# A two-layer RWKV-7 and neighbourhood-attention trunk: ungated heads, spread scalings, a tile of its own for the last scaling

## The chip, the cores and the metric

The kernel runs on one core of one Trainium2 chip. The metric is device time in microseconds (us): the median of several runs of the whole program, less being better. Beside the runs there is one execution recorded by the hardware profiler, and every duration and wait below comes from that recording.

The engines go by short names: PE is TensorE (matmuls and transposes), PEld its weight loads, DVE is VectorE, ACT is ScalarE, POOL is GpSimd, SP is SyncE, and SPq in a row is SP's queue that issues DMAs. Each engine works through its own list of instructions strictly in order; engines wait for each other by semaphores. SBUF is the on-chip memory that tiles live in, PSUM the banks that PE writes its sums to.

## What is computed

Two samples of 512 tokens and 1024 features (the prompt, s=0, and the sample, s=1) go through the same two layers. Cut to what matters here:

```python
def _trunk(x, ...):
    for i in range(DEPTH):                       # 2 layers
        xn = _rms_norm(x, pre_norm_g[i])
        h = _rwkv7_branch(xn, ...) if i % 2 == 0 else _natten_branch(xn, ...)
        x = x + _rms_norm(h, post_norm_g[i])
    return x

def _natten_branch(xn, w_in, b_in, rpb, w_o, b_o):
    q, k, v, z = jnp.split(xn @ w_in + b_in, 4, axis=-1)
    o = _neighbourhood_attention(q * HEAD_DIM ** -0.5, k, v, rpb)   # 16 heads of 64
    return (o * jax.nn.silu(z)) @ w_o + b_o
```

The gate `silu(z)` multiplies the attention's output elementwise, before the output product with `w_o`. The RMS norm after it needs the sum of squares over all 1024 features of a token, so the last scaling of a sample can't begin before its last output column is there.

## The kernel before

**Products.** Every large product is made in fp32 out of pairs of rounded halves: the operand x is `hi + lo`, and one 128x512 step of a product is three matmuls (hi·hi, hi·lo, lo·hi; L429 to L431 in `gemm`). Eight steps, 24 matmuls, make one output column of 128 features for 512 tokens. The weights arrive as raw tiles by DMA (three buffers, `NRAW`), ACT casts each to its `hi` half (L378) and DVE subtracts to get `lo` (L379, both in `halves`); four buffers each hold the halves of the streamed weights.

**Order.** The first part of the program, to about 1075 us, holds the recurrent scans and the first layer's products and is ordered by hand; the change leaves its order alone. What follows is emitted as interleaved Python generators and put in order by the framework's scheduler, which simulates the engines and takes the ready instruction of the highest priority; `high_priority(n)` and `later(n)` shift that priority, and `behind(a, b)` orders instruction a after b. The DMA issues of SP are ordered in the same way, loads and stores in one queue.

**The second layer**, for a sample s:

- `inproj`/`qkvz`: for each of eight pairs of heads p, four columns q, k, v, z. A column is summed in one of two PSUM banks, `pg`. For s=1 DVE moves it out of the bank, multiplied by the norm's factor `x1_rstd` (held in `vs`; L1380), ACT adds the bias (L1384, L1386, L1388, or for z a tanh and an identity, L1391 and L1392), DVE makes the gate (L1394), and SP stores the column to DRAM. At the end of s=1 the columns come in the order q6 k6 v6 q7 k7 v7 z6 z7.
- `heads(s, p)`: loads q, k, v and the bias; v is transposed (L1413, copied by ACT at L1414); for two halves of the queries, scores into one of two PSUM banks `sc` (L1427), softmax on DVE and ACT (L1437 to L1443, the exponential being ACT's L1441), transposes of the probabilities into one of two PSUM banks `pt` (L1447), copies of these to `pts` by ACT (L1450), and the product with v back into the same `sc` bank (L1471). Before the second half's product the generator stays put until column z of this pair has been emitted. Then L1485 multiplies the result straight out of PSUM by z, which SP has loaded (`z<-dz`). For s=1 the gated output is split into halves (`os`).
- `out1(0)`: sample 0's output product: eight columns of 24 matmuls; then the norm (`rstd`, L460 to L469), and for each of eight columns a load of the residual `xr`, the scaling (L1511), the addition (L1512) and the store of y (L1513). PE works by then on sample 1's columns.
- `by_token`: sample 1's residual is transposed (L1523), copied (L1525) and stored.
- `last()`: sample 1's output product with tokens on the partitions, so that the norm is along a row: all 16 tiles of `w_ao` are loaded and split first, then for two halves c of the features and four groups m of tokens 24 matmuls (L1565 to L1567). `LAST[m]` gives the bank, `pg` or `pt` by turns. DVE adds the bias (L1569), ACT squares and sums (L1570), DVE multiplies by the norm's weight in place (L1571); for c=1 then the two sums (L1574), square root (L1575), reciprocal (L1576), two scalings with the residual added (L1578), and two stores by SP (L1579).

Tiles that matter below: `tmp` is a rotating set of five 128x512 buffers, and `oa` and `os` hold columns through the end. A tile may be written again only when its last reader has finished.

Of the kernel before, what the change touches and what calls it, by code (L numbers as in the profile page):

```python
# [10 lines left out]
F32 = mybir.dt.float32  # L11
# [7 lines left out]
P = 128  # L19
T = 512  # L20
# [217 lines left out]
class Trunk:  # L238
    NACT, NW, NRAW, NXR, NTMP, WP = 18, 4, 3, 3, 5, 512
    POST0, POST, POST2, POST3, NPA = 0.7, 1.0, 0.15, 0.66, 5  # L240
    HP, HS = (1000, 0), 1000
# [13 lines left out]
    NA = 1000  # L255
    SUMS, SG, ZY = 0, 0, 2
# [119 lines left out]
    def halves(self, src, lo, hi, eng=None):  # L376

        self.nc.scalar.copy(hi, src)  # L378
        (eng or self.nc.vector).tensor_tensor(lo, src, hi.bitcast(F32), op=ALU.subtract)  # L379
        return hi, lo  # L380
# [907 lines left out]
    def norm0(self, s):  # L1288

        nc = self.nc  # L1290
        rstd = self.h_acc
        yield from self.rstds(rstd)
        acc = self.t("vs", bufs=self.NVS)
        for k in range(KT):
            h = self.h[k]
            x = self.load(self.t("xr", bufs=self.NXR), self.a["xc"][s][k * P:(k + 1) * P, :])
            nc.vector.scalar_tensor_tensor(h, h, self.vec("post0", k), rstd, op0=ALU.mult, op1=ALU.mult)
            nc.vector.tensor_tensor(h, h, x, op=ALU.add)
            nc.scalar.activation(x, h, AF.Square)
# [73 lines left out]
    def qkvz(self, s, p, c, ps):  # L1373
# [4 lines left out]
        if s:  # L1378
            yield first("D")
            vt.tensor_tensor(o, ps, self.x1_rstd, op=ALU.mult)  # L1380
# [16 lines left out]
    def heads(self, s, p):  # L1397
# [19 lines left out]
        left, z = [], []  # L1417
        for ns in ((0, 1), (2, 3)):
# [34 lines left out]
            if ns[1] == 3:  # L1453
                while ("z1", s, p) not in self.sp:
                    yield
# [22 lines left out]
            left.append((sc, slice(ns[0] * P, ns[0] * P + 2 * P)))  # L1478
            yield
            if ("z1", s, p) in self.sp:  # L1480
                if not z:
                    z.append(self.load(b("z1"), self.sp["z1", s, p]))
                for sc, at in left:
                    with self.tc.high_priority(self.HP[s] if p == NP - 1 else 0):
                        vt.tensor_tensor(  # L1485
                            o[:, at].rearrange("p (n t) -> p n t", n=2), sc[:, :, 2 * NKEY:],
                            z[0][:, at].rearrange("p (n t) -> p n t", n=2), op=ALU.mult)
                left = []
# [7 lines left out]
    def out1(self, s):  # L1496
        nc = self.nc
        x = self.operands(lambda k: self.os[s][k])
        acc = self.t("acc1", pool=self.ap)
# [8 lines left out]
        rstd = self.rstd(acc)  # L1508
        for k, h in enumerate(hs):
            x = self.load(self.t("xr", bufs=self.NXR), self.sp["x1", s, k])  # L1510
            nc.vector.scalar_tensor_tensor(h, h, self.vec("post1", k), rstd, op0=ALU.mult, op1=ALU.mult)  # L1511
            (nc.vector if k % 2 else nc.vector).tensor_tensor(h, h, x, op=ALU.add)  # L1512
            nc.sync.dma_start(self.a["y"][s][k * P:(k + 1) * P, :], h)  # L1513
            yield
# [14 lines left out]
    def last(self):  # L1529
# [27 lines left out]
        for c in range(2):  # L1557
            cs = slice(c * T, c * T + T)
            for m in range(4):
# [3 lines left out]
                for k in range(KT):  # L1563
                    (xh, xl), (wh, wl) = self.os[1][k], w[c][k]
                    nc.tensor.matmul(ps, xh[:, ms], wh, start=(k == 0), stop=False)  # L1565
                    nc.tensor.matmul(ps, xh[:, ms], wl, start=False, stop=False)
                    nc.tensor.matmul(ps, xl[:, ms], wh, start=False, stop=(k == KT - 1))  # L1567
                hs[c, m] = h = self.t("oa", (P, T), NP, F32, self.ap)
                vt.tensor_tensor(h, ps, row["bo"][:, cs], op=ALU.add)  # L1569
                act.activation(self.tmp(), h, AF.Square, accum_out=st[:, m, c:c + 1])  # L1570
                (vt if c and m == 3 else vt).tensor_tensor(h, h, row["post1"][:, cs], op=ALU.mult)  # L1571
                if c:
# [4 lines left out]
                    for j in range(2):  # L1577
                        vt.scalar_tensor_tensor(hs[j, m], hs[j, m], r, xt[j], op0=ALU.mult, op1=ALU.add)  # L1578
                        nc.sync.dma_start(self.a["y"][1][ms, j * T:j * T + T], hs[j, m])  # L1579
# [343 lines left out]
```

## Time and profile before

| what | value |
|---|---|
| runs | 1678.75, 1676.94, 1675.66 us |
| their median | 1676.94 us |
| the profiled execution | 1671.44 us |
| its span, first to last instruction | 1669.6 us |
| mean granted TensorE clock of the span | 0.961 |
| DMA over the span | 326.86 MB, mean 196 GB/s |

How to read the profile: a row of a timeline gives the start, the duration, the engine, the line of the kernel, what it wrote and read, how many instructions it holds, and in square brackets for how long the engine had been idle and what it waited for. Matmuls overlap, so the step from one start to the next is a matmul's cost, not its duration. A row of the windows gives, for a stretch of the span, each engine's busy time and instructions, the clock granted to PE as a share of full speed, and the DMA engines' busy share. A row of the waits gives: the waiting engine, tile and line, what it waited for, the total, the number of times, and the longest. Some matmul records are missing, so counts in windows are lower bounds.

### The profile page before, as it was taken

What the parts mean: (1) busy time and instruction counts of PE and PEld (TensorE: products, weight loads), DVE (VectorE), ACT (ScalarE), POOL (GpSimd) and SP (SyncE); (2) the same over time, 40 slices, a digit from 0 to 9 for tenths busy, and PEclk for the clock granted to TensorE, in tenths of its full rate; (3) what the DMA queues carried; (4) which work ended last, traced back from release to release, by engine and by line L of the source; (5) the groups of instructions that cost most, each with busy time, mean ns of one, the idle gap of its engine ahead of it and who ended that gap; (6) DMA issues with size and microseconds to landing.
All of it is one profiled execution on the core that took longest, in us unless ns stands there. A gap on an engine that the chain in (4) does not pass through costs nothing.

```text
span 1669.6 us, 46734 instructions
## 1 busy us (share of the span) xinstructions
PE 1523.9 (91%) x19072; PEld 1168.3 (70%) x19072; DVE 1183.1 (71%) x2661; ACT 968.5 (58%) x2001; POOL 20.6 (1%) x64
## 2 busy tenths in 40 slices
PE   7989777987998898889889989999999999999988
PEld 6867555765665676676667766788777787777766
DVE  8985788777887887968788987343456686555654
ACT  5444665756757575566856555444566665454552
POOL 0000000000000000000000000000000000000000
PEclk9989987998999999999899999999999999999999
DMA  5435786777775767768774656574565347655552
GB/s 210 164 126 178 239 285 204 220 228 240 223 227 190 215 217 238 231 191 254 217 234 158 219 172 212 162 242 159 172 197 176 93 145 249 190 166 172 157 159 101
DMA packets 247096, 326.86 MB, mean 196 GB/s; under 512 B 54849, under 2 KB 132801, under 8 KB 246881
## 3 DMA queue, kind: packets, MB, share of 16 engines
q1 hardware_dynamic: 246880, 323.87, 61.0%
q8 instruction: 150, 2.46, 0.6%
q14 instruction: 66, 0.53, 0.1%
HBM read 220.37 MB, written 103.42 MB: 194 GB/s over the span
## 4 chain that ended last, share of the span: by engine, by line
PE 48%; DVE 10%; ACT 9%; DMA 5%; issue 3%; SPq 1%; DVEq 0%; ACTq 0%
PE pg L430 6%; PE pg L429 6%; PE pg L431 6%; PE pm L763 5%; PE pm L764 4%; PE pm L765 4%; DMA cab<-dab 2%; PE sc L1471 2%; PE pf L1080 2%; PE sc L1427 1%; PE pt L1447 1%; PE zy L1157 1%; PE us L1171 1%; DVE ab L844 1%; PE zy L1126 1%
## 5 line engine op out<-in xcount | busy, mean ns | idle before, releaser
L763 PE MATMUL pm<-act,whi 128*128 128x512 f32 x608 | 269.5, 443 | 21.1 <-ACT act L746 14.7
L764 PE MATMUL pm<-act,whi 128*128 128x512 f32 x608 | 247.5, 407 | 15.5 <-DVE act L748 14.0
L765 PE MATMUL pm<-act,wlo 128*128 128x512 f32 x608 | 245.5, 404 | 0.3 <-DVE wlo L726 0.2
L429 PE MATMUL pg<-act,whi 128*128 128x512 f32 x480 | 192.9, 403 | 2.8 <-DVE tmp L1380 1.9
L430 PE MATMUL pg<-act,whi 128*128 128x512 f32 x480 | 191.4, 399 | 0.0
L431 PE MATMUL pg<-act,wlo 128*128 128x512 f32 x480 | 190.8, 398 | 0.0
L379 DVE TENSOR_TENSOR wlo<-raw,whi 128x512 fp32r<-128x512 f32 x156 | 107.0, 688 | 86.1 <-ACT whi L378 81.2
L378 ACT CAST whi<-raw 128x512 fp32r<-128x512 f32 x156 | 96.4, 618 | 114.6 <-PE pg L430 68.5
L763 PEld LDWEIGHTS pm<-act,whi 128*128 128x128 f32 x608 | 118.2, 194 | 62.4 <-ACT act L746 17.0
L764 PEld LDWEIGHTS pm<-act,whi 128*128 128x128 f32 x608 | 119.1, 196 | 42.0 <-DVE act L748 19.0
L726 DVE TENSOR_TENSOR wlo<-raw,whi 128x512 fp32r<-128x512 f32 x152 | 103.3, 686 | 56.4 <-ACT whi L724 56.2
L765 PEld LDWEIGHTS pm<-act,wlo 128*128 128x128 f32 x608 | 118.7, 195 | 28.2 <-DVE wlo L726 2.1
L724 ACT CAST whi<-raw 128x512 fp32r<-128x512 f32 x152 | 92.6, 619 | 77.6 <-PE pm L764 65.6
L429 PEld LDWEIGHTS pg<-act,whi 128*128 128x128 f32 x480 | 90.6, 189 | 21.5 <-DVE tmp L1380 2.1
L430 PEld LDWEIGHTS pg<-act,whi 128*128 128x128 f32 x480 | 90.8, 189 | 19.4 <-issue 2.0
L431 PEld LDWEIGHTS pg<-act,wlo 128*128 128x128 f32 x480 | 90.7, 189 | 19.5 <-issue 1.7
L970 DVE TENSOR_TENSOR N<-etmp,N 128x30 f32<-128x30 f32 (+14 forms) x240 | 79.8, 333 | 8.2
L1080 PE MATMUL pf<-cab 64*64 64x128 f32 (+1 forms) x2048 | 72.0, 271 | 12.1 <-issue 6.6
L969 DVE TENSOR_TENSOR etmp<-N 128x30 f32<-128x30 f32 (+14 forms) x240 | 78.2, 326 | 3.4
L1166 ACT COPY X<-zy 64x256 f32<-64x256 f32 x128 | 46.9, 366 | 46.8 <-PE zy L1157 41.1
L1441 ACT ACTIVATE sb<-sb,mx 128x192 f32<-128x192 f32 x128 | 57.1, 449 | 24.7 <-DVE mx L1440 24.5
L1080 PEld LDWEIGHTS pf<-cab 64*64 64x64 f32 x2048 | 57.6, 136 | 18.7 <-issue 8.9
(400 smaller groups left out, 3188.5 us busy)
## 6 DMA issues: line engine op xcount, KB each, us to landing
dab<-ab SPq DMA_DIRECT2D x32, 1024.0 KB
cab<-dab SPq DMA_DIRECT2D x64, 512.0 KB
raw<-in_w_in_dram SPq DMA_DIRECT2D x128, 256.0 KB
raw<-in_w_z_dram SPq DMA_DIRECT2D x32, 256.0 KB
dz<-tmp SPq DMA_DIRECT2D x32, 256.0 KB
raw<-in_w_k_dram SPq DMA_DIRECT2D x32, 256.0 KB
dk<-tmp SPq DMA_DIRECT2D x32, 256.0 KB
raw<-in_w_r_dram SPq DMA_DIRECT2D x32, 256.0 KB
```

Of the source, the lines that this page charges most:

```text
L378: self.nc.scalar.copy(hi, src)
L379: (eng or self.nc.vector).tensor_tensor(lo, src, hi.bitcast(F32), op=ALU.subtract)
L429: nc.tensor.matmul(ps, hi, x[k][0], start=(k == 0), stop=False)
L430: nc.tensor.matmul(ps, hi, x[k][1], start=False, stop=False)
L431: nc.tensor.matmul(ps, lo, x[k][0], start=False, stop=(k == KT - 1))
L724: nc.scalar.copy(hi, raw[h])
L726: nc.vector.tensor_tensor(lo, raw.pop(h), hi.bitcast(F32), op=ALU.subtract)
L763: nc.tensor.matmul(ps, hi[:, at], xh, start=(k == 0), stop=False)
L764: nc.tensor.matmul(ps, hi[:, at], xl, start=False, stop=False)
L765: nc.tensor.matmul(ps, lo[:, at], xh, start=False, stop=(k == KT - 1))
L970: vt.tensor_tensor(N[:, q + 1:, :q], tv, N[:, q + 1:, :q], op=ALU.add)
L1080: end = nc.tensor.matmul(f[half(1 - a), h, 0, d, g] if st.last else f[half(1 - a), h, :, d, g], ab[half(h), d, g, 2 * e[d] + a], rt if st. ...
```

## The change

Five things, all after 1075 us:

1. **Heads without their gate leave PSUM ungated.** `heads` no longer waits for column z between the two halves. If z has not been emitted when a half's product is there, ACT copies the product out of `sc` as it is, and one multiply over all 512 columns follows in SBUF once z is there. Otherwise the multiply out of PSUM stays.
2. **Sample 0's last scalings are spread.** `out1(0)` waits until three of sample 1's columns have been moved out of PSUM; each load, scaling, addition and store is then given a lower priority (`OUT_LATER`), and each scaling is ordered behind the latest such move (`self.evac`).
3. **The last scaling has its own tile.** For c=1, the square writes its unused elementwise result into the PSUM bank instead of a `tmp`; the multiply by the norm's weight writes to a `tmp` rather than in place, for c=1. The first matmul of the two last groups is ordered behind the end of the group before. The very last store is issued by ACT.
4. Sample 0's last pair of heads (p=7) gets priority 3000 in place of 1000.
5. `norm0`'s scalings from the second on are ordered behind the split of sample 0's operands (`self.joint`).

```diff
-    HP, HS = (1000, 0), 1000
+    HP, HS = (3000, 0), 3000
+    OUT_LATER = 1500
...
-            nc.vector.scalar_tensor_tensor(h, h, self.vec("post0", k), rstd, op0=ALU.mult, op1=ALU.mult)
+            normed = nc.vector.scalar_tensor_tensor(h, h, self.vec("post0", k), rstd, op0=ALU.mult, op1=ALU.mult)
+            if k:
+                self.behind(normed, self.joint)
...
-            vt.tensor_tensor(o, ps, self.x1_rstd, op=ALU.mult)
+            self.evac = vt.tensor_tensor(o, ps, self.x1_rstd, op=ALU.mult)
+            self.did["evac"] += 1
...
-            if ns[1] == 3:
-                while ("z1", s, p) not in self.sp:
-                    yield
...
+            at = slice(ns[0] * P, ns[0] * P + 2 * P)
+            ov, gate = (x[:, at].rearrange("p (n t) -> p n t", n=2) if x is not None else None for x in (o, z()))
+            with self.tc.high_priority(self.HP[s] if p == NP - 1 else 0):
+                if gate is None:
+                    act.copy(ov, sc[:, :, 2 * NKEY:])
+                    left.append(at)
+                else:
+                    vt.tensor_tensor(ov, sc[:, :, 2 * NKEY:], gate, op=ALU.mult)
+        while left and z() is None:
+            yield
+        if left:
+            at = slice(left[0].start, left[-1].stop)
+            with self.tc.high_priority(self.HP[s] if p == NP - 1 else 0):
+                vt.tensor_tensor(o[:, at], o[:, at], z()[:, at], op=ALU.mult)
...
         rstd = self.rstd(acc)
+        while self.did["evac"] < 3:
+            yield
         for k, h in enumerate(hs):
-            x = self.load(self.t("xr", bufs=self.NXR), self.sp["x1", s, k])
-            nc.vector.scalar_tensor_tensor(h, h, self.vec("post1", k), rstd, op0=ALU.mult, op1=ALU.mult)
-            (nc.vector if k % 2 else nc.vector).tensor_tensor(h, h, x, op=ALU.add)
-            nc.sync.dma_start(self.a["y"][s][k * P:(k + 1) * P, :], h)
+            with self.later(self.OUT_LATER):
+                x = self.load(self.t("xr", bufs=self.NXR), self.sp["x1", s, k])
+                self.behind(nc.vector.scalar_tensor_tensor(h, h, self.vec("post1", k), rstd, op0=ALU.mult, op1=ALU.mult), self.evac)
+                nc.vector.tensor_tensor(h, h, x, op=ALU.add)
+                nc.sync.dma_start(self.a["y"][s][k * P:(k + 1) * P, :], h)
...
+                    if c and m > 1 and k == 0:
+                        self.behind(begun, ended)
...
-                act.activation(self.tmp(), h, AF.Square, accum_out=st[:, m, c:c + 1])
-                (vt if c and m == 3 else vt).tensor_tensor(h, h, row["post1"][:, cs], op=ALU.mult)
+                act.activation(ps if c else self.tmp(), h, AF.Square, accum_out=st[:, m, c:c + 1])
+                hs[c, m] = self.tmp() if c else h
+                vt.tensor_tensor(hs[c, m], h, row["post1"][:, cs], op=ALU.mult)
...
-                        nc.sync.dma_start(self.a["y"][1][ms, j * T:j * T + T], hs[j, m])
+                        (act if m == 3 and j else nc.sync).dma_start(self.a["y"][1][ms, j * T:j * T + T], hs[j, m])
```

What it does to the built order is shown at two places. Line numbers of the changed kernel are a little higher: L379 becomes L380, L1380 becomes L1383, L1511 and L1512 become L1526 and L1527, L1441 becomes L1451, L1450 becomes L1460; L1490 is the new copy.

**The middle, on DVE**, where sample 0's output product has ended and sample 1's first columns run (`os` are sample 0's eight output columns, `wlo` the halves of the next weights, the `pg` banks hold columns k0 and v0). Before:

```order
L379 TENSOR_TENSOR wlo_18739<-raw_18732,whi_18738 128x512
L1511 SCALAR_TENSOR_TENSOR os_18125<-os_18125,cv,acc_3095_18080 128x512
...
L1511 SCALAR_TENSOR_TENSOR os_18496<-os_18496,cv,acc_3095_18080 128x512
L1512 TENSOR_TENSOR os_18125<-os_18125,xr_18596 128x512
L1512 TENSOR_TENSOR os_18176<-os_18176,xr_18649 128x512
L1512 TENSOR_TENSOR os_18238<-os_18238,xr_18699 128x512
L379 TENSOR_TENSOR wlo_18803<-raw_18798,whi_18802 128x512
L1380 TENSOR_TENSOR tmp_18669<-pg_18621,vs_18182 128x512
L1380 TENSOR_TENSOR tmp_18725<-pg_18686,vs_18182 128x512
```

And in the changed kernel, the same place:

```order
L380 TENSOR_TENSOR wlo_18724<-raw_18717,whi_18723 128x512
L380 TENSOR_TENSOR wlo_18788<-raw_18783,whi_18787 128x512
L1383 TENSOR_TENSOR tmp_18659<-pg_18616,vs_18182 128x512
L1383 TENSOR_TENSOR tmp_18710<-pg_18676,vs_18182 128x512
L1526 SCALAR_TENSOR_TENSOR os_18125<-os_18125,cv,acc_3095_18080 128x512
L380 TENSOR_TENSOR wlo_18792<-raw_18785,whi_18791 128x512
L1527 TENSOR_TENSOR os_18125<-os_18125,xr_18746 128x512
L380 TENSOR_TENSOR wlo_18898<-raw_18893,whi_18897 128x512
L1383 TENSOR_TENSOR tmp_18775<-pg_18727,vs_18182 128x512
L1526 SCALAR_TENSOR_TENSOR os_18176<-os_18176,cv,acc_3095_18080 128x512
```

The two moves out of `pg` stood behind eight scalings and three additions; now they stand ahead of all of them, and one scaling and one addition follow each later move. On SP's queue the eight stores of y, which stood within 25 rows, are spread over 53 in the same way, each among the loads of weights.

**The tail, on PE**, where the last pair of heads (1,7) meets the last columns (`sc_20928`/`sc_20929` is the second half of pair (1,6); `sc_21139`/`sc_21129` the first half of pair (1,7); `pg_21366`/`pg_21367` is the first sum of `last()`). Before, the second half of pair 6, then z6's last steps and the whole of z7, 18 matmuls of `last()`, and only then the scores:

```order
L1471 MATMUL sc_20928<-pts_20963,vtok_20784 64x64
L431 MATMUL pg_21011<-act_18531,wlo_21008 128x512
...
L1567 MATMUL pg_21366<-act_21300,os_20756 128x512
L1427 MATMUL sc_21139<-k_3762_21102,q_3761_21100 64x192 x8
L1427 MATMUL sc_21201<-k_3762_21102,q_3761_21100 64x192 x8
```

In the changed kernel the scores stand within z6 and z7:

```order
L1437 MATMUL sc_21129<-k_3762_21097,q_3761_21095 64x192
L1478 MATMUL sc_20929<-pts_21019,vtok_20784 64x64
...
L1437 MATMUL sc_21129<-k_3762_21097,q_3761_21095 64x192 x7
L432 MATMUL pg_21012<-act_18527,wlo_21009 128x512
...
L432 MATMUL pg_21079<-act_18511,wlo_21072 128x512
L1437 MATMUL sc_21202<-k_3762_21097,q_3761_21095 64x192 x8
L430 MATMUL pg_21079<-act_18515,whi_21071 128x512
```

The first scores of pair 7 moved up by 43 matmuls of 512 columns, the second by 30.

**The tail, on ACT**, where the halves of the last tiles of `w_ao` are cast (`whi_213..`, the 13th to 16th of 16) and pair 7's probabilities are copied to `pts`. Before:

```order
L378 CAST whi_21360<-raw_21361 128x512
L1441 ACTIVATE sb_21149,mx_21150<-sb_21149,mx_21150 128x192
...
L1441 ACTIVATE sb_21230,mx_21237<-sb_21230,mx_21237 128x192
L1450 COPY pts_21165<-pt_21148 128x384
L1450 COPY pts_21184<-pt_21167 128x384
L1450 COPY pts_21227<-pt_21210 128x384
L1450 COPY pts_21246<-pt_21229 128x384
```

In the changed kernel, where the eight exponentials stand further up, among the casts of the sixth to tenth tile:

```order
L1460 COPY pts_21166<-pt_21138 128x384
L1460 COPY pts_21185<-pt_21168 128x384
L379 CAST os_21064<-tmp_20810 128x512
L379 CAST whi_21343<-raw_21344 128x512
L379 CAST whi_21349<-raw_21350 128x512
L379 CAST whi_21355<-raw_21356 128x512
L379 CAST whi_21361<-raw_21362 128x512
L1460 COPY pts_21228<-pt_21211 128x384
L1460 COPY pts_21247<-pt_21230 128x384
```

All of pair 7's exponentials and half of its copies now stand ahead of the last casts, and the other half of the copies still behind them. In the whole program the ungated way out (two copies L1490, one multiply L1499) is taken by pair (1,6) alone.

More of the change, by code (lines that the diff above doesn't have):

```diff
@@ L378, in halves @@
         self.nc.scalar.copy(hi, src)
-        (eng or self.nc.vector).tensor_tensor(lo, src, hi.bitcast(F32), op=ALU.subtract)
+        self.parted = (eng or self.nc.vector).tensor_tensor(lo, src, hi.bitcast(F32), op=ALU.subtract)
         return hi, lo
@@ L1416, in heads, with z @@
         o = self.tmp() if s else self.t("oa", (P, T), NP, F32, self.ap)
-        left, z = [], []
+        left, gates = [], []
+        def z():
+            if not gates and ("z1", s, p) in self.sp:
+                gates.append(self.load(b("z1"), self.sp["z1", s, p]))
+            return gates[0] if gates else None
         for ns in ((0, 1), (2, 3)):
@@ L1477, in heads @@
                                 self.behind(av, first)
-            left.append((sc, slice(ns[0] * P, ns[0] * P + 2 * P)))
             yield
[L1480 to L1488, printed above, removed]
+            at = slice(ns[0] * P, ns[0] * P + 2 * P)
[12 more added lines that the diff above has]
+                vt.tensor_tensor(o[:, at], o[:, at], z()[:, at], op=ALU.mult)
         with self.tc.high_priority(self.HP[s] if p == NP - 1 else 0):
@@ L1498, in out1 @@
         x = self.operands(lambda k: self.os[s][k])
+        self.joint = self.parted
         acc = self.t("acc1", pool=self.ap)
@@ L1564, in last @@
                     (xh, xl), (wh, wl) = self.os[1][k], w[c][k]
-                    nc.tensor.matmul(ps, xh[:, ms], wh, start=(k == 0), stop=False)
+                    begun = nc.tensor.matmul(ps, xh[:, ms], wh, start=(k == 0), stop=False)
+                    if c and m > 1 and k == 0:
+                        self.behind(begun, ended)
                     nc.tensor.matmul(ps, xh[:, ms], wl, start=False, stop=False)
-                    nc.tensor.matmul(ps, xl[:, ms], wh, start=False, stop=(k == KT - 1))
+                    ended = nc.tensor.matmul(ps, xl[:, ms], wh, start=False, stop=(k == KT - 1))
                 hs[c, m] = h = self.t("oa", (P, T), NP, F32, self.ap)
                 vt.tensor_tensor(h, ps, row["bo"][:, cs], op=ALU.add)
-                act.activation(self.tmp(), h, AF.Square, accum_out=st[:, m, c:c + 1])
-                (vt if c and m == 3 else vt).tensor_tensor(h, h, row["post1"][:, cs], op=ALU.mult)
+                act.activation(ps if c else self.tmp(), h, AF.Square, accum_out=st[:, m, c:c + 1])
+                hs[c, m] = self.tmp() if c else h
+                vt.tensor_tensor(hs[c, m], h, row["post1"][:, cs], op=ALU.mult)
                 if c:
```

## The prediction

> **What bounds the kernel now.** I read the page's first part, then the windows, the waits of PE from 1050 us on, and the timelines at the waits. First the page, and six windows of 10 us (PE, PEld, DVE, ACT, POOL, granted clock, DMA share, GB/s):
>
> ```profile
> PE 1523.9 (91%) x19072; PEld 1168.3 (70%) x19072; DVE 1183.1 (71%) x2661; ACT 968.5 (58%) x2001; POOL 20.6 (1%) x64
> ```
> ```profile
> 1380.00:1390.00 10.00, 10.00 (x57) 8.55 (x55) 7.73 (x15) 4.42 (x8) 0.00 (x0) 1.00 0.49 160
> 1390.00:1400.00 10.00, 8.13 (x34) 6.43 (x33) 6.62 (x11) 4.61 (x8) 0.00 (x0) 0.83 0.89 312
> 1410.00:1420.00 10.00, 9.01 (x49) 7.43 (x48) 7.29 (x40) 8.46 (x26) 0.00 (x0) 1.00 0.60 189
> 1610.00:1620.00 10.00, 8.07 (x58) 5.77 (x59) 8.98 (x36) 7.16 (x19) 0.00 (x0) 1.00 0.51 151
> 1620.00:1630.00 10.00, 8.42 (x54) 6.50 (x54) 2.81 (x17) 2.93 (x10) 0.00 (x0) 0.83 0.07 23
> 1660.00:1670.00 10.00, 2.20 (x10) 1.45 (x8) 3.96 (x8) 1.01 (x3) 0.00 (x0) 0.72 0.28 105
> ```
>
> PE sets the time. Where it is full, as at 1380, only fewer matmuls would help, and the change takes none away; it can win only where PE falls short: the five other rows. What PE waits for there, by tile and line (total, times, longest):
>
> ```profile
> PE sc L1427 <- DVE tmp L1485: 2.4, 1, 2.4
> PE pg L429 <- DVE tmp L1380: 1.9, 1, 1.9
> PE pt L1447 <- DVE sb L1443: 1.5, 3, 1.1
> PE pt L1447 <- ACT pts L1450: 1.4, 1, 1.4
> ...
> PE pt L1523 <- ACT tmp L1525: 1.0, 1, 1.0
> ...
> PE pt L1413 <- DMA v<-dv: 0.7, 1, 0.7
> ```
>
> The second and fifth of these lie in the middle, at 1394 and 1416; the others in the tail, 1600 to 1625. After PE's last matmul comes the end, 1662 to 1670.
>
> **Part 1, the spread scalings (middle).** The timeline of DVE, then that of PE:
>
> ```profile
> 1385.63 5.39 DVE L1511 SCALAR_TENSOR_TENSOR os<-os,cv,acc 128x512 f32<-128x512 f32 x8 [0.84 <-ACT acc L469]
> 1390.93 1.90 DVE L1512 TENSOR_TENSOR os<-os,xr 128x512 f32<-128x512 f32 x3
> ...
> 1393.34 1.29 DVE L1380 TENSOR_TENSOR tmp<-pg,vs 128x512 f32<-128x512 f32 x2
> ```
> ```profile
> 1391.62 0.60 PE L1523 MATMUL pt<-cc,hh 128*128 128x128 f32 x4
> 1394.09 0.50 PE L429 MATMUL pg<-act,whi 128*128 128x512 f32 x1 [1.87 <-DVE tmp L1380]
> ...
> 1394.66 0.54 PE L431 MATMUL pg<-act,wlo 128*128 128x512 f32 x1
> ...
> 1398.53 0.40 PE L429 MATMUL pg<-act,whi 128*128 128x512 f32 x1
> 1398.77 0.39 PE L430 MATMUL pg<-act,whi 128*128 128x512 f32 x1
> ```
>
> Eight scalings and three additions, 5.39 + 1.90 = 7.29 us, stand in DVE's queue ahead of the two moves out of `pg`. Both banks are full, so column z0 waits 1.87 us for the first move. Then PE is slow: the 10 steps from 1394.66 to 1398.53 take 3.87 us, 0.39 each, against 0.24 for the step at 1398.53. At 0.23 (the tail's steps, below) they would be 2.3 us: 1.57 us lost to the clock after the wait. In the new order both moves stand ahead of the first scaling, so the wait goes (1.87), and with it, I take it, the slow stretch (1.57). The third term is the wait of 0.99 us at 1416, where a transpose finds its bank not yet copied by ACT:
>
> ```profile
> 1416.50 0.66 PE L1523 MATMUL pt<-cc,hh 128*128 128x128 f32 x4 [0.99 <-ACT tmp L1525]
> ```
>
> ACT is then at 8.46 of 10 with the softmax of sample 1's first pair. That work starts some 3 us earlier in the new order, the transposes being spread out further, so I count the wait as gone. Sum: 1.87 + 1.57 + 0.99 = 4.4 us; if ACT is as crowded as before, 3.4; if only the wait itself is won, 1.9.
>
> What is moved costs this. The 16 scalings and additions, 0.67 us each by the row of eight (5.39 / 8), now come one pair a column behind a move: 1.3 us of DVE for each column of 24 x 0.23 = 5.5 us. DVE is at 7.7 of 10 in the full window at 1380, with eight scalings partly in it; queued behind such a pair are the halves of the next weights, held back by at most 1.3 us, and four buffers stand between these and PE. Cover enough: nothing. The loads of `xr` and stores of y on SP's queue are moved too: each store waits for its addition, and raw weights stand behind it. That is a rival below. The DMA share of 0.89 at 1390 to 1400 rather falls when the stores spread.
>
> [...]
>
> **Part 2, ungated heads (tail).** PE's timeline, with the DVE and DMA rows that released it:
>
> ```profile
> 1607.50 0.34 SPq L334 DMA_DIRECT2D z<-dz  x1
> ```
> ```profile
> 1607.91 0.40 PE L1567 MATMUL pg<-act,os 128*128 128x512 f32 x1
> 1610.71 1.53 PE L1427 MATMUL sc<-k,q 64*64 64x192 f32 x32 [2.41 <-DVE tmp L1485]
> ...
> 1619.49 0.97 PE L1447 MATMUL pt<-cc,sb 128*128 128x128 f32 x4 [1.07 <-DVE sb L1443]
> 1620.64 0.44 PE L1447 MATMUL pt<-cc,sb 128*128 128x128 f32 x2 [0.18 <-DVE sb L1443]
> 1622.48 0.55 PE L1447 MATMUL pt<-cc,sb 128*128 128x128 f32 x3 [1.40 <-ACT pts L1450]
> ...
> 1624.79 0.78 PE L1565 MATMUL pt<-h,os 128*128 128x512 f32 x1
> ...
> 1626.98 0.39 PE L1567 MATMUL pt<-h,os 128*128 128x512 f32 x1
> ...
> 1661.81 0.40 PE L1567 MATMUL pt<-whi,os 128*128 128x512 f32 x1
> ```
>
> Pair 7's scores wait 2.41 us for `sc`, which pair 6 holds until z6 has gone to DRAM and come back. Then its softmax and copies come late, and PE waits 1.07 + 0.18 + 1.40 us. With the 0.7 for v (the last row of the waits): 5.7 us. At 1624.79 starts the sum in a `pt` bank. From the order, 150 of the 192 matmuls of `last()` are left then, and 12 small products. The five steps to 1626.98 take 2.19 us, 0.44 each, double the rest: (1661.81 - 1626.98) is 34.83 us for 145 - 1 steps and the products, of some 1.2 us: 0.23 each. So 2.19 - 5 x 0.23 = 1.0 us more is lost to the clock.
>
> After the change the same PE work stands ahead of that `pt` sum (42 matmuls of `last()`, 16 score matmuls, 12 transposes, 12 products in either order). If nothing waited but v, PE would be there at 1624.79 - 5.06 - about 1 (slow steps on the way) = 1618.7. But ACT frees `sc` now: a copy of 128x256 out of PSUM is
>
> ```profile
> L1185 ACT COPY y<-zy 128x256 f32<-128x256 f32 x32 | 11.8, 369 | 5.5 <-PE zy L1175 5.1 <-DVE AK L1059 0.3
> ```
>
> 0.37 us, and the second of these stands behind two or three casts that wait for raw tiles; I take 0.6 us of wait for PE. And the bank itself: it is free only when `pts` has been copied, and that copy stands behind the casts of tiles 13 to 16:
>
> ```profile
> 1590.37 0.62 ACT L378 CAST h<-raw 128x512 fp32r<-128x512 f32 x1 [4.11 <-DMA raw<-in_w_ao_dram]
> ...
> 1616.98 0.62 ACT L378 CAST whi<-raw 128x512 fp32r<-128x512 f32 x1 [1.08 <-DMA raw<-in_w_ao_dram]
> ```
> ```profile
> L1441 ACT ACTIVATE sb<-sb,mx 128x192 f32<-128x192 f32 x128 | 57.1, 449 | 24.7 <-DVE mx L1440 24.5
> ```
>
> The 16 tiles come through three raw buffers, one each (1616.98 - 1590.37) / 15 = 1.77 us, a cast being 0.62: ACT and DVE hold the buffer, the load fills it, and any wait of ACT is passed on to the next load. Ahead of the last cast now stand, beyond what stood there before, eight exponentials (8 x 0.45 = 3.6 us), two copies to `pts` and two ungated copies (some 1.6 us): 5.2 us. All of it in ACT's waits for raw tiles would cost nothing, and the cast ends at 1617.6 as before; all of it in series, 1622.8. I take two thirds, since the exponentials in turn wait for DVE: 1621.1. The first copy to `pts` ends 0.5 us later, and the sum starts at 1621.6 instead of 1624.79: **3.2 us**. PE then waits some 2 to 3 us ahead of it, as long as the waits that are gone, so the 1.0 us of slow steps stays. Bounds: 0 (cast at 1624.3) to 6.1 + 1.0.
>
> **Part 3, the end.** The last columns' rows on DVE, and SP's:
>
> ```profile
> 1662.24 0.69 DVE L1569 TENSOR_TENSOR oa<-pt,rbo 128x512 f32<-128x512 f32 x1 [1.31 <-PE pt L1567]
> 1663.78 0.69 DVE L1571 TENSOR_TENSOR oa<-oa,rpost 128x512 f32<-128x512 f32 x1 [0.85 <-ACT tmp L1570]
> 1664.39 0.15 DVE L1574 TENSOR_TENSOR st<-st 128x1 f32<-128x1 f32 x1
> ```
> ```profile
> 1660.29 6.58 SPq L1579 DMA_DIRECT2D out_dram<-oa  x4
> ```
>
> L1571 writes in place and so waits for ACT's square to have read. With a tile of its own it runs beside the square, and L1574 comes when the square is done, 1663.78 rather than 1664.39: **0.6 us**. The square's write to PSUM has no row; its nearest is any ACT row, and I take 0 (-0.1 to 0.1). The last store, issued by ACT beside SP: I take 0 (-0.3 to 0.3), since SP's issues end with the span in either case.
>
> **Parts 4 and 5.** Sample 0's last pair and `norm0`: the order around them hardly moves, and PE has no wait there in the list: 0 (-0.3 to 0.3).
>
> **Sum:** 4.4 + 3.2 + 0.6 = 8.2 us. The profiled execution of 1671.44 becomes 1663.2. The median of the runs shown, 1676.94, is 5.5 us above it; I keep that distance: **1668.7 us**.
>
> **The rivals.**
> - *The tail's stream isn't slowed.* ACT has the room (7.16 of 10 at 1610): the exponentials fit in its waits. Then PE is at the `pt` sum at 1618.7 with no wait, or 0.6 later: 5.5 to 6.1, and the slow steps go, 1.0. Total 4.4 + 6.8 + 0.6 = 11.8: 1665.1. Chance 0.15.
> - *The clock isn't won in the middle.* The slow steps come of something else than the wait, say of the transposes and the thin PE work around it, which stay. Then part 1 is 2.9 and the total 6.7: 1670.2. For: the clock row at 1390 mixes both. Against: the slow steps begin right at the wait. Chance 0.05. [...]
> - *The middle's gain is given back.* Column z0 no longer waits, but the first pair's q, k, v must be stored and reloaded through the same queue, and PE waits for them or for the transposes' bank a few columns on. Then 0 + 3.8: 1673.1. Chance 0.12.
> - *Slower: SP's queue.* Eight stores of y now stand between loads of raw weights, and each holds the queue until its addition is done. If a raw load comes later than its column by more than the buffers cover, PE waits, once a column, eight times. For: DVE is at 7.3 to 7.7 of 10 there, and the addition stands behind a move, a scaling and one or two halves, 2.6 us. Against: PE is full at 1380 with raw loads behind such stores too, and a column lasts 5.5 us. It decides when each of the eight costs over 8.2 / 8 = 1.0 us; at 1.6 us each, 12.8 is lost and 8.2 won: 1681.5. Chance 0.06, with whatever else makes it slower.
> - *It does nothing.* The scheduler's order isn't the engines': pair 7's products wait for z7 in either case, and the middle's wait moves to the raw tiles. Gains of 0 to 3: 1674 to 1677. Chance 0.09.
>
> **How the numbers follow.** The forecast has 0.53. A measurement of this kernel can tell 0.2%, 3.4 us, from no change: faster ends at 1673.6. Faster: the forecast, the first two rivals, and most of the third (0.11 of 0.12): 0.84. The same: 0.10, slower 0.06. The range: from 1663.5, below the first rival with its 0.3s, to 1674.0, above the third; it leaves out the last two, and the tail's lowest bound with the highest of the middle.
>
> **What would show it.** Right: no wait of `pg` on L1383 near 1394 and granted clock 1.00 there; window 1410 full; scores at L1437 without a 2.4 us wait; a wait of a `pt` bank for `pts` L1460 ahead of `last()`'s third sum; L1589 directly behind L1586. Wrong: a new wait of `pg` or for raw weights or v between 1390 and 1450; casts of `w_ao` ending after 1624; waits of `sc` on L1490 above 1 us.

## The result, and the profile after

Over 18 runs each, the changed kernel has a median of 1667.22 us and the kernel before 1672.53 us, 5.3 us apart. One run of each was far longer, 2826.66 and 2081.42 us; the means of the other 17 are 1665.10 and 1673.59 us, a ratio of 0.9949 with a 95% interval of 0.9925 to 0.9974: faster by 0.51%, or 8.5 us (4.3 to 12.5). The forecast was 1668.7 us, a ratio of 0.9951 to the median known then.

The profiled executions alone would have hidden this. The span after is 1670.1 us, before 1669.6. The cause lies ahead of the change: the last gating of the first layer, the last row `bv<-bv,dv,sz` on DVE ("the second multiply by sz" in the expectations below), comes at 1102.79 us before and at 1108.36 after, though nothing was reordered up to there. Over the 14 profiles of this study that row lies between 1095.28 and 1108.36. So I count every stage from this row on, and call it the scans' end. The span's end is read to 0.1 us, so counts that reach to it are good to 0.05 us.

| stage, us | before | after |
|---|---|---|
| scans' end to the move of column z1 out of PSUM | 327.52 | 324.04 |
| on to the move of the fourth-last column | 152.12 | 152.61 |
| on to the first sum of `last()` in a `pt` bank | 42.36 | 40.30 |
| on to the end of PE's last matmul | 37.42 | 37.95 |
| on to the end of the span | 7.39 | 6.84 |
| scans' end to the end | 566.81 | 561.74 |

The windows of after that answer to those of before (all rows are 5.6 us later by the scans alone):

```profile
1390.00:1400.00 10.00, 10.00 (x58) 8.56 (x57) 3.75 (x6) 5.72 (x10) 0.00 (x0) 1.00 0.75 251
1410.00:1420.00 10.00, 10.00 (x54) 8.40 (x53) 9.36 (x45) 8.40 (x26) 0.00 (x0) 1.00 0.64 194
1610.00:1620.00 10.00, 9.89 (x69) 7.69 (x68) 7.15 (x20) 7.12 (x18) 0.00 (x0) 1.00 0.69 202
1620.00:1630.00 10.00, 6.20 (x21) 4.62 (x20) 2.77 (x5) 2.32 (x5) 0.00 (x0) 0.83 0.29 89
```

The middle is full, at full clock (1400 to 1410, into which column z0 falls here, is as full); the tail's loss has moved out of 1610 and gathered in 1620. The waits of PE after 1050 us show it as one row:

```profile
PE pt L1580 <- ACT pts L1460: 3.8, 1, 3.8
...
PE pt L1417 <- DMA v<-dv: 0.8, 1, 0.8
...
PE pt L1457 <- DVE sb L1453: 0.4, 1, 0.4
```

The middle on PE, then on DVE: column z0 begins at 1398.39, right behind the transposes with no wait, since the bank that it takes was moved out at 1395.70. The next move out of `pg`, at 1398.24, waits for PE rather than PE for it, with a single scaling behind it.

```profile
1398.04 0.60 PE L1538 MATMUL pt<-cc,h 128*128 128x128 f32 x4
1398.39 0.49 PE L430 MATMUL pg<-act,whi 128*128 128x512 f32 x1
1398.72 0.39 PE L431 MATMUL pg<-act,whi 128*128 128x512 f32 x1
1398.95 0.39 PE L432 MATMUL pg<-act,wlo 128*128 128x512 f32 x1
```
```profile
1395.70 0.68 DVE L1383 TENSOR_TENSOR tmp<-pg,vs 128x512 f32<-128x512 f32 x1
1398.24 0.69 DVE L1383 TENSOR_TENSOR tmp<-pg,vs 128x512 f32<-128x512 f32 x1 [1.86 <-PE pg L432]
1398.85 0.74 DVE L1526 SCALAR_TENSOR_TENSOR os<-os,cv,acc 128x512 f32<-128x512 f32 x1
```

The tail, on PE and on ACT. The first sum in a `pt` bank waits 3.80 us for a copy to `pts`, and that copy stands behind two casts that wait for raw tiles. Then matmuls start 0.43 us apart until 1629.24, at a granted clock of 0.50 from 1625.93 to 1629.34.

```profile
1621.12 0.39 PE L1584 MATMUL pg<-act,os 128*128 128x512 f32 x1
1625.31 0.50 PE L1580 MATMUL pt<-h,os 128*128 128x512 f32 x1 [3.80 <-ACT pts L1460]
...
1626.26 0.63 PE L1580 MATMUL pt<-h,os 128*128 128x512 f32 x1
1626.68 0.63 PE L1583 MATMUL pt<-h,os 128*128 128x512 f32 x1
...
1629.24 0.44 PE L1583 MATMUL pt<-hh,os 128*128 128x512 f32 x1
```
```profile
1623.47 0.62 ACT L379 CAST whi<-raw 128x512 fp32r<-128x512 f32 x1 [3.14 <-DMA raw<-in_w_ao_dram]
1624.26 0.62 ACT L379 CAST whi<-raw 128x512 fp32r<-128x512 f32 x1 [0.18 <-DMA raw<-in_w_ao_dram]
1624.79 0.85 ACT L1460 COPY pts<-pt 128x384 f32<-128x384 f32 x2
```

The end on DVE, and ACT's queue: the multiply follows the move at once, and the sum of squares comes 1.54 us after the move's start (1664.84 - 1663.30), 2.15 before (1664.39 - 1662.24).

```profile
1663.30 0.69 DVE L1586 TENSOR_TENSOR oa<-pt,rbo 128x512 f32<-128x512 f32 x1 [1.98 <-PE pt L1584]
1664.02 0.69 DVE L1589 TENSOR_TENSOR tmp<-oa,rpost 128x512 f32<-128x512 f32 x1
...
1664.84 0.16 DVE L1592 TENSOR_TENSOR st<-st 128x1 f32<-128x1 f32 x1
```
```profile
1667.01 0.37 ACTq L1597 DMA_DIRECT2D out_dram<-tmp  x1
```

### The profile page after: what moved, and what is told of

Read it like the earlier page. It is cut to its first block, busy times and chain, and to the rows that moved or that the text cites. A ratio compares the mean times of both kernels' runs of the same rounds, so it can differ in the third digit from the quotient of the medians.

```text
span 1670.1 us, 46716 instructions
## 1 busy us (share of the span) xinstructions
PE 1533.1 (92%) x19072; PEld 1176.8 (70%) x19072; DVE 1184.4 (71%) x2660; ACT 968.5 (58%) x2003; POOL 20.7 (1%) x64
## 4 chain that ended last, share of the span: by engine, by line
PE 52%; ACT 8%; DVE 8%; DMA 4%; issue 3%; DVEq 0%; ACTq 0%; SPq 0%
PE pg L431 6%; PE pg L430 6%; PE pg L432 6%; PE pm L764 5%; PE pm L765 5%; PE pm L766 5%; PE pf L1081 2%; DMA cab<-dab 2%; PE sc L1437 2%; PE sc L1478 1%; PE pt L1457 1%; PE zy L1127 1%; PE zy L1158 1%; PE us L1172 1%; ACT X L1167 1%
## 5 line engine op out<-in xcount | busy, mean ns | idle before, releaser
L380 DVE TENSOR_TENSOR wlo<-raw,whi 128x512 fp32r<-128x512 f32 x156 | 106.9, 687 | 88.1 <-ACT whi L379 80.8
L764 PEld LDWEIGHTS pm<-act,whi 128*128 128x128 f32 x608 | 119.9, 197 | 62.2 <-ACT act L747 16.2
L379 ACT CAST whi<-raw 128x512 fp32r<-128x512 f32 x156 | 96.3, 618 | 111.0 <-PE pg L431 62.3
L765 PEld LDWEIGHTS pm<-act,whi 128*128 128x128 f32 x608 | 120.9, 199 | 42.8 <-DVE act L749 19.1
L1451 ACT ACTIVATE sb<-sb,mx 128x192 f32<-128x192 f32 x128 | 57.0, 448 | 26.3 <-DVE mx L1450 26.2
```

Source lines behind the costliest of these rows:

```text
L380: self.parted = (eng or self.nc.vector).tensor_tensor(lo, src, hi.bitcast(F32), op=ALU.subtract)
L764: nc.tensor.matmul(ps, hi[:, at], xh, start=(k == 0), stop=False)
L765: nc.tensor.matmul(ps, hi[:, at], xl, start=False, stop=False)
```

## The experiments

Each kernel below has one profile. Since total times of one kernel spread over some 20 us, the stages are compared; timed rounds are given where there were several. "The tail" is the stretch from the fourth-last column's move to PE's last matmul.

**1. The spread scalings alone.** The kernel before with `out1` as in the change (without `self.joint`) and the two lines in `qkvz`.

```diff
+        while self.did["evac"] < 3:
+            yield
         for k, h in enumerate(hs):
+            with self.later(self.OUT_LATER):
...
+                self.behind(nc.vector.scalar_tensor_tensor(...), self.evac)
```

> The kernel before with only sample 0's last scalings spread. I count from the second multiply by sz on DVE, where the scans' part is over (1102.79 us in the profile before, 1108.36 after), to the end of the span: 566.8 us before, 561.7 after. Theory (the two moves out of pg behind eight scalings are the cause of the wait at 1394 and of the slow steps behind it): no wait of pg for L1380's move, the columns from z1 on 4.4 to 4.8 us earlier against the first column's move, the tail as before; the count is 562.0 to 562.4. Rival (the slow steps come of the clock's own phase and not of the wait): only 1.9 to 2.9 us, 563.9 to 564.9. Rival (the work that moved is paid for later, at raw weights or in a full DVE): under 1.5 us by the last column.

Measured: 324.16 us to z1's move, as in after, with no wait of `pg` and no slow steps. But on to the fourth-last column it took 156.02 instead of 152.1 to 152.6, and the whole came to 565.24. The loss is one place, PE's wait, SP's load and the window around it:

```profile
1423.38 0.55 PE L1429 MATMUL sc<-k,q 64*64 64x192 f32 x6 [1.70 <-DMA xr<-dx]
```
```profile
1417.29 0.40 SPq L335 DMA_DIRECT2D k<-dk  x1
```
```profile
1415.00:1425.00 10.00, 8.30 (x84) 6.21 (x86) 6.32 (x10) 3.87 (x7) 0.00 (x0) 0.98 0.96 337
```

The scores of sample 1's second pair need k. Its load is issued at 1417.29, behind stores of y, loads of `xr` and raw tiles, into DMA engines that are 0.96 busy; the scores start 6.1 us after the issue and 1.70 late. (The row names the `xr` load, which landed about then; that k is meant is my reading.) Slow steps follow. In after, the order on all engines here is the same, and the scores start 6.0 us after the issue without waiting. So the middle's gain is real and can be given back in an execution: 3.4 us in one of the six profiles with this spreading.

**2. The ungated heads alone.** The kernel before with `heads` as in the change.

```diff
+                if gate is None:
+                    act.copy(ov, sc[:, :, 2 * NKEY:])
+                    left.append(at)
```

> The kernel before with only the ungated way out of PSUM for heads without their gate. Theory (the tail's waits are traded for one wait of the pt bank on the copies to pts behind the casts of the last four tiles): the middle as before, with its 1.87 us wait; no 2.4 us wait of scores for sc; a wait of 3 to 4 us ahead of the first sum of the last product that lies in a pt bank; that sum 2 to 3 us earlier against the last columns than before; the count from the second multiply by sz to the end 563.8 to 565.3 (566.8 before). Rival (the tail's gain needs the earlier middle, since loads come earlier there too): the sum no earlier, 566 to 567.

Measured: whole 567.02, no gain. The `sc` wait is gone, the new wait is there, and PE's waits also show that of column z0:

```profile
PE pt L1572 <- ACT pts L1456: 3.3, 1, 3.3
PE pt L1530 <- ACT tmp L1532: 2.2, 1, 2.2
PE pg L429 <- DVE tmp L1380: 1.9, 1, 1.9
```

The sum in the `pt` bank came 2.9 us earlier (39.48 us behind the fourth-last column, before 42.36), but after it 11 steps ran at 0.43 us: 38.88 us to the last matmul against 37.42. Here the middle lost too: 329.16 to z1's move, with the transposes' wait at 2.16 us. My figure for the whole failed on the slow steps, which I had priced as in before.

**3. The last product alone.** The kernel before with `last()` as in the change.

```diff
-                act.activation(self.tmp(), h, AF.Square, accum_out=st[:, m, c:c + 1])
+                act.activation(ps if c else self.tmp(), h, AF.Square, accum_out=st[:, m, c:c + 1])
+                hs[c, m] = self.tmp() if c else h
```

> The kernel before with only the changes in the last product: the square into PSUM and the last scaling's own tile for the second half, the ordering of the last two groups, the last store by ScalarE. Theory: all up to the end of the last matmul as before; from there to the end of the span 6.8 us in place of 7.4, the 0.6 being the multiply that no longer waits for the square. Rival (the store by ScalarE or the square's write to PSUM has a part in it): the step from the move out of PSUM to the sum of squares, or from the last scaling to the end of the span, differs from before by over 0.15 us, and the 0.6 is made of other pieces.

Measured: 6.85 us from PE's end to the end. On DVE the steps are those of after: multiply right behind the move, sum 1.54 us after the move's start.

```profile
1656.08 0.69 DVE L1571 TENSOR_TENSOR oa<-pt,rbo 128x512 f32<-128x512 f32 x1 [1.98 <-PE pt L1569]
1656.80 0.69 DVE L1574 TENSOR_TENSOR tmp<-oa,rpost 128x512 f32<-128x512 f32 x1
1657.62 0.16 DVE L1577 TENSOR_TENSOR st<-st 128x1 f32<-128x1 f32 x1
```

From the end of the last scaling (1659.01 + 0.74) to the end of the span (1662.9) it is 3.15 us; before, 1669.6 - 1666.51 = 3.09. So ACT's store gave nothing, and the 0.6 is the multiply. The tail, whose code is that of before but for the order of two groups, took 77.22 us against 79.78: the profile that I had forecast from lay at the upper end there.

**4. The old priorities.** The changed kernel without parts 4 and 5.

```diff
-    HP, HS = (3000, 0), 3000
+    HP, HS = (1000, 0), 1000
...
-            if k:
-                self.behind(normed, self.joint)
```

> The changed kernel with the old priorities of sample 0's last pair and of its output product's first step, and without the ordering behind the split operands. In the profile after, sample 0's output product starts 1.4 us later against the scans' end than in the profile before (offset of 5.5 us at 1295, 6.9 us at 1337). Theory (it is the order: the last pair's scores stand 1.3 us further back): the offset at 1337 is that at 1295 within 0.3, and the count from the second multiply by sz to the end is 1.0 to 1.4 us below that of after (561.7): 560.3 to 560.7. Rival (it is the clock, which happened to be halved behind the 1 us wait at the norm): the scores' place makes no difference, and the offset differs only by whether steps behind the norm run at 0.43 or 0.23 us: 0 or 0.9 us.

Measured: 323.63 us to z1's move, whole 560.79. The profile of after has 324.04 and 561.74, its repetition (below) 324.76 and 561.13. The differences, 0.95 and 0.34 us of the whole, are about that of the two profiles of one kernel (0.61), so parts 4 and 5 are not shown to do anything. The clock sides with the rival: behind the norm's wait of 1.05 us the granted clock is 0.50 for 3.41 us in after (from 1339.2) and here (from 1328.3), and 1.00 behind that wait, there 1.06 us, in the profile before.

**5. Copies ahead of the casts.** The changed kernel, with the casts of the last four tiles ordered behind pair 7's copies to `pts`.

```diff
-                act.copy(pts[-1], pt)
+                self.copied = act.copy(pts[-1], pt)
...
                 w[c].append(self.halves(raw, lo, hi, self.alt(k)))
+                if c and k > 3:
+                    self.behind(self.cast, self.copied)
```

> The changed kernel with the casts of the last four tiles of w_ao ordered behind the last pair's copies to pts. Counts run from the second multiply by sz on DVE. In the four tails with the old way out or the new one, the time from the fourth-last column's move out of PSUM to PE's last matmul is 77.2 to 79.8 us (old way: 79.8, 77.6, 77.2; new way: 78.3, 78.4, 77.7): the tail gained nothing that stands out, since the new way's one wait of 3.3 to 3.8 us is followed by 1.5 to 2.8 us of slow steps. Theory (that wait and the clock behind it ate the tail's gain, and the copies stand behind casts that wait for raw tiles): the wait of the pt bank falls below 0.7 us, no slow steps follow, and the stretch is 72.5 to 74.0 us; the whole count is 556 to 558 (561.7 in after). Rival (the raw tiles come late whatever the order on ScalarE, so the wait turns into one of the last product for its weights): the stretch stays above 76.5.

Measured: the tail 72.66 us, the whole 556.10; over three rounds 0.9914 of the kernel before (0.9885 to 0.9942). On ACT the copies now come as soon as PE has the transposes, and the last cast, 520.4 us behind the scans' end in place of 515.9, keeps nobody waiting; in the windows PE is full:

```profile
1606.13 0.84 ACT L1460 COPY pts<-pt 128x384 f32<-128x384 f32 x2
...
1608.38 0.86 ACT L1460 COPY pts<-pt 128x384 f32<-128x384 f32 x2 [0.89 <-PE pt L1457]
1609.14 1.14 ACT L379 CAST whi<-raw 128x512 fp32r<-128x512 f32 x2
...
1618.13 0.62 ACT L379 CAST whi<-raw 128x512 fp32r<-128x512 f32 x1 [5.39 <-DMA raw<-in_w_ao_dram]
```
```profile
1610.00:1620.00 10.00, 10.00 (x64) 7.82 (x63) 3.25 (x6) 1.68 (x4) 0.00 (x0) 1.00 0.20 55
1620.00:1630.00 10.00, 10.00 (x44) 7.72 (x43) 5.67 (x9) 3.16 (x9) 0.00 (x0) 1.00 0.35 107
```

So the order of two kinds of instruction on ACT had held the tail's gain.

**6. No scalings at all.** The changed kernel with sample 0's eight columns stored unscaled, without the loads of `xr`, the scalings and the additions.

```diff
-                x = self.load(self.t("xr", bufs=self.NXR), self.sp["x1", s, k])
-                self.behind(nc.vector.scalar_tensor_tensor(...), self.evac)
-                nc.vector.tensor_tensor(h, h, x, op=ALU.add)
                 nc.sync.dma_start(self.a["y"][s][k * P:(k + 1) * P, :], h)
```

> The changed kernel without sample 0's last scalings, additions and loads of the residual; its eight columns are stored as they are. Theory (spread, they cost PE nothing but the 0.5 us that the stretch from z1 to the fourth-last column grew in all three kernels that spread them, and now and then a wait of the second pair's scores for k, 1.7 us and as much again of slow steps, as in the kernel with the scalings spread alone): from the scans' end to z1's move 323.4 to 324.2 us (323.6 to 324.2 with them; 327.5 to 329.2 before), from z1 to the fourth-last column 152.1 in place of 152.6. Rival (the spread scalings cost more, say the moves out of PSUM queued behind them): z1's move comes 1 us or more earlier than with them.

Measured: 324.41 us to z1's move, 0.2 above the range, and 152.81 on to the fourth-last column. Spread, the scalings cost PE nothing that shows. The half microsecond that the second stretch grew (152.12 to 152.61) stays without them, so it isn't theirs, against what I had expected. The traces put it in one place: from the move of v2 to that of q3, two columns on, it is 14.63 us before and 15.09 after, while the same two columns of the next three pairs take 15.10 in both, and PE has no wait there in either. PE's order differs there: the second half's scores start 3.5 us behind the first half's before and 4.6 after. That this order is the cause isn't shown.

**7 and 8. Both kernels again,** unedited.

> The changed kernel as it is, for a second profile. Theory: from the scans' end to z1's move 323.5 to 324.5 us, 152.6 to the fourth-last column unless the second pair's scores wait for k (then up to 156.0), 77.5 to 78.5 to PE's last matmul with a wait of 3 to 4 us ahead of the first sum in a pt bank and 1.5 to 2.8 us of slow steps behind it, 6.85 to the end. Rival (the profile of after was an unlucky one): a tail below 76.5.

> The kernel before as it is, for a second profile. Theory: 327.5 to 329.2 us from the scans' end to z1's move, with the wait of 1.9 for column z0 and slow steps behind it; 152.1 to the fourth-last column; 77.2 to 79.8 to PE's last matmul; 7.4 to the end. Rival (the slow steps behind the 1.9 us wait come and go with the clock's phase): the wait is there without them, and the first figure is 326 or less.

Measured, after: 324.76, 152.61, tail 76.87 (a wait of 3.65 us, 6 slow steps), 6.89; whole 561.13. Before: 328.62, 153.02, tail 79.10, 7.44; whole 568.18, with the wait of 1.87 and 7 slow steps behind it. Three ranges were missed: after's first stretch by 0.3 us (above) and its tail by 0.6 (below), and the second stretch of before by 0.9 (above, with a wait of 0.57 us for v and 0.17 of others in it).

**9. One batch, behind the moves.** The kernel before, where the eight scalings stay together but wait for the third move out of `pg`.

```diff
+        while self.did["evac"] < 3:
+            yield
         for k, h in enumerate(hs):
...
+            self.behind(nc.vector.scalar_tensor_tensor(...), third if k else self.evac)
+            third = third if k else self.evac
```

> The kernel before with one change: sample 0's last scalings wait until sample 1's third column has been moved out of PSUM and stand behind that move, but all eight still stand together, with the additions right behind. Counts run from the second multiply by sz on DVE. Theory (the place of the two moves is what counts; a batch behind them, 5.4 us of scalings and 1.9 of additions, is covered by the next column's 5.5 us and the two banks): the 1.9 us wait of column z0 is gone and z1's move comes at 323.6 to 325 us, as with the spread scalings (323.6 to 324.8; 327.5 to 329.2 before). Rival (spreading is what counts: a batch of eight holds the next moves or the halves of the weights wherever it stands): a new wait of over 1 us between column z0 and column z1, for a move out of pg or for a wlo, and z1's move at 325.5 or later.

Measured: 325.07 us to z1's move. The wait of z0 is gone, and another has come, at 1414 (PE's waits, then DVE):

```profile
PE pg L429 <- DVE tmp L1380: 1.2, 1, 1.2
```
```profile
1408.86 0.69 DVE L1516 TENSOR_TENSOR os<-os,xr 128x512 f32<-128x512 f32 x1 [2.11 <-DMA xr<-dx]
...
1412.57 0.69 DVE L1516 TENSOR_TENSOR os<-os,xr 128x512 f32<-128x512 f32 x1
...
1413.59 0.68 DVE L1380 TENSOR_TENSOR tmp<-pg,vs 128x512 f32<-128x512 f32 x1
```

Additions that have waited for `xr` meet the first pair's softmax on DVE, and the move stands behind both. Neither expectation is met whole: moving the batch gives 3.2 of the 4.3 us, and spreading it the rest.

**10. Copies ahead of the casts, heads gated.** The kernel before with the edit of 5.

> The kernel before, heads gated as before, with the casts of the last four tiles of w_ao behind the last pair's copies to pts. Theory (the ungated way out is needed for the tail's gain: here the scores still wait 2.3 to 2.7 us for sc, and the copies come late anyway): from the fourth-last column's move to PE's last matmul 76.5 to 80 us, as before (77.2 to 79.8). Rival (the order of copies and casts does it alone): below 75.

Measured: a tail of 75.65 us, between the two expectations. PE's waits:

```profile
PE sc L1427 <- DVE tmp L1485: 2.6, 1, 2.6
...
PE pt L1447 <- ACT pts L1450: 0.2, 1, 0.2
```

The 1.4 us for `pts` is gone without ungated heads, while the 2.6 us for `sc` is not. The middle, unchanged, lost more than before (329.60) through the transposes' wait of 1.96 us.

**11. Copies ahead of the casts, heads ungated, nothing else.** The kernel before with the edits of 2 and 5.

> The kernel before with the ungated way out for heads and the casts of the last four tiles behind the last pair's copies; scalings and last product as before. Theory: the tail needs just these two: from the fourth-last column's move to PE's last matmul 72.4 to 73.6 us (72.7 in the changed kernel with the casts put behind). Rival (the tail's gain there also came of what the spread scalings moved, or of the clock's luck): above 75.

Measured: a tail of 72.07 us, just under the range; whole 558.64. These two edits make the tail, whatever the middle does.

**12. All of it, with the old priorities.** The changed kernel with the edits of 4 and 5.

> The changed kernel with the casts of the last four tiles behind the last pair's copies, with the old priorities of sample 0's last pair and without the ordering behind the split operands. Theory (priorities and that ordering make no difference that shows): the count from the second multiply by sz to the end 555.3 to 556.5 us (556.1 with the new priorities), the ratio to the kernel before 0.991 within 0.003. Rival (the old priorities are better by 0.9 us, as the first profile of after against old priorities suggested): 555.2 or less.

Measured: whole 555.73 us, tail 72.62, and over five rounds 0.9912 of the kernel before (0.9883 to 0.9940; medians 1652.46 and 1669.47). The priorities make no difference here either. This version and that of 5 beat both kernels: against after's 561.1 to 561.7 the count is 5 to 6 us lower.

## Why the prediction was right, and which of its terms were not

The total was right in sign and size: a ratio of 0.9949 where 0.9951 was forecast. By the profiles the gain is 6.1 us (the mean of the two whole counts of before, 567.5, less that of after, 561.4) where the sum said 8.2; the interval of the runs, 4.3 to 12.5, holds both. That the two ratios agree to 0.0002 is luck, then.

**Part 1, 4.4 us: right.** Six profiles with before's middle (before twice, 2, 3, 10, 11) have a mean of 328.30 us to z1's move, six with the spread scalings (after twice, 1, 4, 5, 12) 324.04: 4.3 us. The mechanism is shown by 9: the two moves ahead of the batch take the wait away, though a batch needs spreading too. The wait of 0.99 us at the transposes, counted as gone, is 0.9 to 2.2 us in all six and in none with the spreading. That the moved work costs nothing is shown by 6.

**Its clock term, 1.57 us: right on average, wrong as a rule.** The same 1.87 us wait was followed by 7 or 8 slow steps in four of the six profiles of before's middle. In the other two (2 and 10) it was followed by none, as here in 2:

```profile
1387.03 0.50 PE L429 MATMUL pg<-act,whi 128*128 128x512 f32 x1 [1.87 <-DVE tmp L1380]
1387.37 0.40 PE L430 MATMUL pg<-act,whi 128*128 128x512 f32 x1
1387.60 0.40 PE L431 MATMUL pg<-act,wlo 128*128 128x512 f32 x1
```

In just these two the slow steps came some 22 us later, 7 and 8 of them, behind the transposes' wait of 2.16 and 1.96 us. So each of the six had one such stretch, in the profile before 3.41 us at a granted clock of 0.50 (1394.76 to 1398.17), which costs some 1.6 us (8 steps of 0.43 in place of 0.23); why at the one place or the other is not shown, and the last section has what was measured of it. The rival that the clock isn't won falls: none of the seven profiles with the spreading or without the scalings, where that wait is missing, has slow steps at column z0.

**Part 2, 3.2 us: the mechanism right, the size wrong.** "The sum starts at 1621.6" is 39.2 us behind the fourth-last column; five profiles with ungated heads and the casts ahead (after twice, 2, 4, 6) have 38.5 to 40.3, mean 39.2. The wait, its bank, and what stands ahead of the copy were as told. (The last cast ends at 1624.88 in after, past the 1624 that was to show a failure, but all its rows are 5.6 us late by the scans.) Two numbers around it failed. The start without the change, 42.4 us, came from one profile; five profiles with gated heads and the old order on ACT (before twice, 1, 3, 9) have a mean of 41.6. And "so the 1.0 us of slow steps stays" did not hold: from that sum to the last matmul these five take 37.0 us on average, and the five with ungated heads 38.1, as a single wait of 3.3 to 3.8 us was followed by 6 to 12 slow steps in four of them. Whole tail: 78.6 to 77.3, a gain of 1.3. What was left there is shown by 5: with the copies ahead of the casts the tail is 72.1 to 72.7.

**Part 3, 0.6 us: right,** 0.56 on average, and by the step named (3). **Parts 4 and 5, nothing: right** within 0.7 (4, 12).

**The rival of SP's queue** did occur, once in six profiles, but as a late k for the scores rather than late raw weights, and at one place rather than eight (1).

**The distance of 5.5 us** between profile and median, kept from three runs, was too large: with 18 runs the median of before is 1672.53, 1.1 above its profile. The absolute forecast landed because two errors met: 3.1 us too much gain against the one profile of before (8.2 for 566.81 - 561.74 = 5.1), and 4.4 too much distance. 1668.7 + 3.1 - 4.4 = 1667.4, where 1667.22 was measured. That, too, was luck.

## What to carry to other kernels

With the change PE's wait of 2.4 us for `sc` was gone, and one of 3.8 us for `pts` had come. So ask which instruction the next buffer's release stands behind, and whether that one waits for a DMA (the casts ahead of that copy waited 3.14 and 0.18 us for raw tiles). An order of two copies against four casts was worth here nearly four times what the ungated heads had won (77.3 to 72.5 us, against 78.6 to 77.3). The two need each other: alone they win 3.0 us (78.6 to 75.65, one profile) and 1.3, together 6.2. And where an unchanged stage spreads over 13 us from run to run, count from a fixed instruction behind it, over several profiles, before pricing a stall from one.

## What the runs showed of the hardware

The length of a wait did not tell by itself whether slow steps stood behind it. Waits of 1.87 us were followed by slow steps in four of six cases, those of 3.3 to 3.8 us in four of five, and that of kernel 6, 3.35 us, by none.

In the profiles before and after, the granted clock has two values, 1.00 and 0.50, and each of its changes (45 before, 51 after) lies within 0.02 us of a whole number of steps of 3.4133 us, fitted to them, behind the first. Counted from the span's start, the changes lie 2.12 us past a multiple of this step before and 1.18 us after. In the profile before, the wait of 1.87 us falls into one such step, in which PE is busy for 1.54 of 3.41 us, and in the next step the granted clock is 0.50 (PEclk, the number behind POOL's):

```profile
1391.35:1394.76 3.41, 1.54 (x11) 1.21 (x10) 3.41 (x7) 2.28 (x5) 0.00 (x0) 1.00 1.02 378
1394.76:1398.17 3.41, 3.41 (x10) 2.64 (x9) 0.47 (x2) 0.65 (x2) 0.00 (x0) 0.50 1.01 314
```

In kernel 2, in stretches of the same length, the same wait lies on both sides of 1386.04, and the granted clock is 1.00 in these two and in the next:

```profile
1382.63:1386.04 3.41, 2.54 (x18) 2.03 (x16) 3.41 (x7) 2.86 (x5) 0.00 (x0) 1.00 0.56 212
1386.04:1389.46 3.42, 2.43 (x11) 1.99 (x12) 2.13 (x4) 1.35 (x3) 0.00 (x0) 1.00 1.01 307
1389.46:1392.87 3.41, 3.41 (x17) 2.83 (x16) 1.29 (x2) 0.89 (x2) 0.00 (x0) 1.00 1.03 375
```

Between 1280 us and PE's last matmul the profiles before and after have two stretches each at 0.50, every one 3.41 us long. In the step ahead of them PE was busy for 1.54 us (before, up to 1394.76), 1.83 (before, up to 1623.45), 2.35 (after, up to 1339.21) and 0.62 (after, up to 1625.93). Behind the step from 1606.39 in the profile before, with PE busy for 1.92 us, the granted clock was 1.00. So the busy time of one step does not sort these cases: 0.50 followed 2.35 us, and 1.00 followed 1.92. That the place of a wait against these steps decides, and is the part of chance in it, is my reading of the two middles above; no run tests it.
